# The four step-size features of a hybrid decoder trunk, computed on four column strips of TensorE

## The chip, the cores and the metric

The kernel runs on one core of a Trainium2 chip. The metric is the device time of one execution in microseconds (us), taken as the median of several runs. PE is TensorE, DVE is VectorE, ACT is ScalarE, POOL is GpSimd and SP is the engine whose queue issues the transfers. All data are fp32 in memory.

## The reference

One inference step runs through a two-layer decoder trunk. There are 1048 tokens: 16 meta tokens, a prompt of 1024 and 8 decode tokens, each with 1024 features. In each layer one input projection feeds three groups of mixers (attention, a diagonal state space called S5, and a Mamba-2 scan called SSD). Its last four columns are the raw step sizes of the four SSD heads:

```python
h = rmsnorm(x, ln1_g)
proj = h @ w_in                        # 1024 -> 1796 columns
q, k, v, u, z, xbc, dtr = split(proj)  # dtr: the last 4 columns
dt = softplus(dtr + ssd_dt_bias)       # step sizes of the 4 SSD heads
cs = cumsum(dt * A)                    # A = -exp(ssd_a_log)
Lmat = exp(segment sums of cs)         # decays inside a chunk
```

After the mixers come an output projection, a second norm and a SwiGLU block of 2816 hidden features.

## The kernel before, in words

Features lie on the 128 partitions and tokens along the free dimension. The tokens are cut into two halves (528 and 520 tokens), and each half into two chunks of 264 or 256 tokens. So a layer has two halves and the kernel goes four times through the input projection. They are called (layer, half): (0,0), (0,1), (1,0) and (1,1).

Precision is kept by splitting. A dense product splits weights and activations each into a rounded fp32r part and a remainder; `mm3` (lines 206 to 213) then issues three fp32r matmuls for each of the eight 128-feature tiles of the contraction. `weights` (lines 176 to 187) loads a 128-column weight tile of 512 KB and splits it on ACT (line 184) and DVE (line 186).

`in_norm` (lines 303 to 316) makes the two parts of x times the norm gain, for each chunk and tile (lines 312 and 313), and the reciprocal norm `rs` of each token. The sum over features for that norm goes through PE at line 242 and comes back as a row at line 255. `in_proj` (lines 318 to 357) walks over the names in `MT` (line 33), one 128-column tile each, and multiplies each product by `rs` on the way out of PSUM (lines 347 and 351). The name "dt" holds the four step-size columns, padded to 128. It has its own weights: `weights_dt` (lines 189 to 199) casts the raw tile twice on ACT and writes the remainder of the four columns into columns 32 to 35. Its loop (lines 334 to 341) issues 16 fp32r matmuls per chunk, all 128 columns wide, copies rows 32 to 35 out on ACT, adds rows 0 to 3 and multiplies by `rs` on DVE. The result of 4 rows is stored to a DRAM buffer.

`ssd` loads these 4 rows back and turns them so that tokens are on partitions: five transposes of 4 rows (lines 891 and 896), then a short DVE chain makes the softplus.

All instructions pass through a list scheduler that runs while the program is built. It goes by program order, lifted where `tc.high_priority` stands, and by a simulated timeline; the order on each engine is then fixed. PE takes matmuls in that order, and SP issues all transfers in that order. Buffers rotate in pools: PSUM has two banks for dense products (`pbig`), three for general use (`pmx`) and three for attention; `st` staging tiles are three, general slots 28. At the top (lines 1486 to 1533) the parts are strung together: in layer 0, (0,0) and (0,1) are mixed with the preparation of S5 and with mixers; in the rest the mixers are woven into the dense SwiGLU work. In program order `in_norm(0,0)`, `in_norm(0,1)` and `in_norm(1,1)` stand ahead of the dense work that runs next, and `in_norm(1,0)` stands behind the output projection of (0,1).

Of the kernel before, what the change touches and what calls it, by code (L numbers as in the profile page):

```python
# [7 lines left out]
F32 = mybir.dt.float32  # L8
F32R = mybir.dt.float32r
BF16 = mybir.dt.bfloat16  # L10
AF = mybir.ActivationFunctionType
ALU = mybir.AluOpType
AX = mybir.AxisListType
# [11 lines left out]
TH = (528, 520)  # L25
T0 = (0, 528)
NPR = (528, 512)
CH = (((0, 264), (264, 528)), ((0, 264), (264, 520)))
# [1 line left out]
NK8 = (66, 64)  # L30
HGROUPS = ((0, 8), (8, 16), (16, 22))
EPS = 1e-6
MT = 'u0 u1 k v q0 q1 q2 q3 xs0 xs1 B C dt z0 z1'.split()


def build(ctx, tc, A):
    nc = tc.nc
    V, S, G, PE = nc.vector, nc.scalar, nc.gpsimd, nc.tensor
# [4 lines left out]
    wp = ctx.enter_context(tc.tile_pool(name="wp", bufs=3))  # L43
    stp = ctx.enter_context(tc.tile_pool(name="stp", bufs=3))
# [10 lines left out]
    def nm(s):  # L55
        uid[0] += 1
        return f"{s}_{uid[0]}"
# [54 lines left out]
    def dram(shape, s):  # L112
        return drp.tile(shape, F32, tag=nm("d" + s), name=nm("d" + s))
# [6 lines left out]
    def load(out, in_):  # L120
        last[0] = nc.sync.dma_start(out=out, in_=in_).ins  # L121
        return last[0]
# [11 lines left out]
    ident = const([128, 128], "id")  # L134
# [32 lines left out]
    x = [None, None]  # L167
# [8 lines left out]
    def weights(src, nk, parts=1):  # L176
        raw = wp.tile([128, 8, 128], F32, tag="wr", name=nm("wr"), bufs=2)
        with tc.high_priority(offset=3000):
            load(raw[:, 0:nk], src)
        wh = wp.tile([128, 8, 128], F32R, tag="wh", name=nm("wh"))  # L180
        wl = wp.tile([128, 8, 128], F32R, tag="wl", name=nm("wl"))
        cuts = [nk * i // parts for i in range(parts + 1)]
        for a, b in zip(cuts, cuts[1:]):
            S.copy(wh[:, a:b], raw[:, a:b])  # L184
        for a, b in zip(cuts, cuts[1:]):
            V.tensor_sub(wl[:, a:b], raw[:, a:b], wh[:, a:b].bitcast(F32))  # L186
        return wh, wl

    def weights_dt(l, mi):

        raw = wp.tile([128, 8, 128], F32, tag="wr", name=nm("wr"), bufs=2)
        with tc.high_priority(offset=3000):
            load(raw, A["w_in"][l, mi])
        wh = wp.tile([128, 8, 128], F32R, tag="wh", name=nm("wh"))
        S.copy(wh, raw)
        wl = wp.tile([128, 8, 128], F32R, tag="wl", name=nm("wl"))
        S.copy(wl, raw)
        V.tensor_sub(wl[:, :, 32:36], raw[:, :, 0:4], wh[:, :, 0:4].bitcast(F32))
        return wh, wl

    def split(dst, cols, src, eng=None):
        h, l = dst[:, 0, cols], dst[:, 1, cols]
        S.copy(h, src)  # L203
# [27 lines left out]
    def rstd_sum(acc, n, scale, out=None):  # L231
        rs = ftp.tile([128, 264], F32, tag="rs", name=nm("rs")) if out is None else out
        S.copy(rs[:, :n], rstd_rows(acc, n, scale))
        return rs
# [52 lines left out]
    P = {}  # L287
    for l in range(DEPTH):
        for hf in range(2):
            T = TH[hf]  # L290
            for n_ in ("xs0", "xs1", "B", "C", "k", "v", "z0", "z1"):
                P[l, hf, n_] = dram([128, T], n_)
            P[l, hf, "dt"] = dram([4, T], "dt")
            P[l, hf, "u"] = dram([2, 128, 8 * NK8[hf]], "u")
            P[l, hf, "ud"] = dram([2, 128, NDEC], "ud")
            P[l, hf, "q"] = dram([4, 128, T], "q")
            P[l, hf, "mixa"] = dram([4, 128, T], "mixa")
            for j in range(4):
                P[l, hf, f"mix{j}"] = P[l, hf, "mixa"][j]
            for j in range(4, 8):  # L300
                P[l, hf, f"mix{j}"] = dram([128, T], "mix")

    def in_norm(l, hf, new):

        xn = [new() for _ in range(8)]
        g = par("ln1", l)
        rs = slot()
        for c0, c1 in CH[hf]:
            acc = None
            for k, t in enumerate(x[hf]):  # L310
                h, lo = xn[k][:, 0, c0:c1], xn[k][:, 1, c0:c1]
                S.activation(h, t[:, c0:c1], AF.Copy, scale=g[:, k:k + 1])
                V.scalar_tensor_tensor(lo, t[:, c0:c1], g[:, k:k + 1], h.bitcast(F32), ALU.mult, ALU.subtract)  # L313
                acc = add_square(acc, t[:, c0:c1], c1 - c0)
            rstd_sum(acc, c1 - c0, 1.0 / D, rs[:, c0:c1])
        return xn, rs

    def in_proj(l, hf, xr, early=0):

        xn, rs = xr  # L320
        bn = [0]
        T = TH[hf]
        nk = NK8[hf]
        for mi, name in enumerate(MT):
            w = weights(A["w_in"][l, mi], 8) if name != "dt" else weights_dt(l, mi)
            st = stp.tile([128, 528], F32, tag="st", name=nm("st"))
            for c0, c1 in CH[hf]:
                n = c1 - c0
                bn[0] += 1
                if mi < early and bn[0] % 2:  # L330
                    ps = mxp.tile([128, 512], F32, tag="xa", name=nm("px"), bufs=PSB["a"])
                else:
                    ps = pbig()
                if name == "dt":
                    for k in range(8):
                        PE.matmul(ps[:, :n], w[1][:, k, :], xn[k][:, 0, c0:c1], start=(k == 0), stop=False)
                        PE.matmul(ps[:, :n], w[0][:, k, :], xn[k][:, 1, c0:c1], start=False, stop=(k == 7))
                    S.copy(st[0:4, c0:c1], ps[32:36, :n])
                    V.tensor_add(st[0:4, c0:c1], st[0:4, c0:c1], ps[0:4, :n])
                    V.tensor_mul(st[0:4, c0:c1], st[0:4, c0:c1], rs[0:4, c0:c1])  # L340
                    continue
                mm3(ps[:, :n], w, xn, c0, c1)
                if name[0] == "u":
                    e = min(c1, NPR[hf])
                    sv = st[:, 0:8 * nk].rearrange("p (s k) -> p k s", s=8)
                    by8 = lambda t: t.rearrange("p (k s) -> p k s", s=8)
                    V.tensor_mul(sv[:, c0 // 8:e // 8, :], by8(ps[:, :e - c0]), by8(rs[:, c0:e]))
                    if e < c1:
                        V.tensor_mul(st[:, e:c1], ps[:, e - c0:n], rs[:, e:c1])
                else:  # L350
                    V.tensor_mul(st[:, c0:c1], ps[:, :n], rs[:, c0:c1])  # L351
            with tc.high_priority(offset=3000):
                if name == "dt":
                    load(P[l, hf, "dt"], st[0:4, :T])
                elif name[0] == "u":
                    load(P[l, hf, "u"][int(name[1])], st[:, :8 * nk])
                    if T > 8 * nk:
                        load(P[l, hf, "ud"][int(name[1])], st[:, 8 * nk:T])
                elif name[0] == "q":
                    load(P[l, hf, "q"][int(name[1])], st[:, :T])  # L360
                else:
                    load(P[l, hf, name], st[:, :T])
            yield
# [469 lines left out]
    def ssd(l, hf):  # L833
        T, NP = TH[hf], NPR[hf]
# [46 lines left out]
        f0 = 16 if hf == 0 else 0  # L881
        blocks += [(f0 + 128 * i, 128, i) for i in range(4)]

        dr = slot()
        load(dr[0:4, :T], P[l, hf, "dt"])
        sm5 = kvp.tile([128, 9, 20], F32, tag="ssds", name=nm("ssds"), bufs=2)
        v_, e_, s_, z_, dt, dA, cs, w_, mx_ = [sm5[:, i, :] for i in range(9)]
        V.memset(v_, 0.0)
        pt = pmx()
        for i in range(4):  # L890
            PE.transpose(pt[:, 4 * i:4 * i + 4], dr[0:4, f0 + 128 * i:f0 + 128 * i + 128], ident[0:4, 0:4])
        V.tensor_copy(v_[:, 0:16], pt[:, 0:16])
        pt2 = pmx()
        ne = 16 if hf == 0 else 8
        o5 = 0 if hf == 0 else NP
        PE.transpose(pt2[0:ne, 0:4], dr[0:4, o5:o5 + ne], ident[0:4, 0:4])
        V.tensor_copy(v_[0:ne, 16:20], pt2[0:ne, 0:4])
        b5 = lambda n: par(n, l).unsqueeze(1).to_broadcast([128, 5, 4])
        f5 = lambda t: t.rearrange("p (b h) -> p b h", h=4)
# [53 lines left out]
        for c0, nq, bi in blocks:  # L953
            cols = slice(c0, c0 + nq)
# [602 lines left out]
def _host(i):  # L1557
    import numpy as np

    c = np.ascontiguousarray  # L1560
    f = np.float32
    r = {}
# [4 lines left out]
    cols = {"k": np.arange(512, 640), "v": np.arange(640, 768), "u0": np.arange(768, 896), "u1": np.arange(896, 1024),  # L1567
            "z0": np.arange(1024, 1152), "z1": np.arange(1152, 1280), "xs0": np.arange(1280, 1408),
            "xs1": np.arange(1408, 1536), "B": np.arange(1536, 1664), "C": np.arange(1664, 1792),
            "dt": np.arange(1792, 1796)}  # L1570
    for j in range(4):
        cols[f"q{j}"] = hp[128 * j:128 * j + 128]
    wcols = {n: i["w_in"][:, :, cols[n]] for n in MT}

    wcols["dt"] = np.concatenate([wcols["dt"], np.zeros((2, 1024, 124), f)], axis=2)

    def tiles(w, nm_):

# [11 lines left out]
    P = {}  # L1590
# [38 lines left out]
    st = np.stack([i["state_s5_re"], i["state_s5_im"]], axis=1)  # L1629
# [75 lines left out]
```

## Time and profile before

| | us |
|---|---|
| median of 3 runs | 2483.13 (2478.48 to 2488.88) |
| the profiled execution | 2487.19 |
| its span, first to last instruction | 2485.3 |
| PE busy in it | 2396.9 (96%) |
| DVE busy | 1463.9 (59%) |
| ACT busy | 1059.1 (43%) |

The rows further down come from that one profiled execution. A matmul's own duration in the trace contains its way through the array, and matmuls overlap; the pace of PE is read from the distance between the starts of neighbours. A plain fp32 product appears as two matmuls in the trace (two passes), a fp32r product or a transpose as one.

### The profile page before, as it was taken

Reading aid. Unit: us, or ns where it says so; the run is one execution under the profiler, and the core shown is the slowest. Engines: PE = TensorE matmul, PEld = TensorE weight load, DVE = VectorE, ACT = ScalarE, POOL = GpSimd, SP = SyncE. Lnnn points to the kernel's source line nnn. Section 1 sums busy time; section 2 is a strip of 40 time slices with the busy share of each in tenths; the row PEclk is TensorE's granted clock in tenths of the full one; section 3 lists DMA queues with packets and bytes.
Section 4 is the critical chain, followed back from the end, with each engine's and each line's share of the span. In section 5 each row is a group of like instructions: output and inputs, shape, how many; then the busy total and the mean of one; then the engine's idle time right before and its main releaser. Section 6 shows DMA issues by size and latency. Waiting matters only on the chain.

```text
span 2485.3 us, 49901 instructions
## 1 busy us (share of the span) xinstructions
PE 2396.9 (96%) x20006; PEld 2312.5 (93%) x20006; DVE 1463.9 (59%) x3502; ACT 1059.1 (43%) x2183; POOL 353.4 (14%) x478
## 2 busy tenths in 40 slices
PE   7999789999999999999999999999999999999997
PEld 7988688999999999999999999999999998999997
DVE  8777557666659655564664545665565447434344
ACT  5455534334543533353554443343454435323234
POOL 6302121011013230001110021001110004000000
PEclk9999899999999999999999999999999999999999
DMA  7555332454324534253432334446432233232322
GB/s 251 189 160 155 99 118 74 127 154 147 91 82 143 182 110 150 77 148 114 129 103 86 100 101 134 121 134 189 139 100 89 84 117 111 95 94 89 99 83 80
DMA packets 202712, 301.09 MB, mean 121 GB/s; under 512 B 55905, under 2 KB 132529, under 8 KB 202449
## 3 DMA queue, kind: packets, MB, share of 16 engines
q1 hardware_dynamic: 202480, 297.91, 38.7%
q8 instruction: 157, 2.57, 0.4%
q14 instruction: 75, 0.61, 0.1%
HBM read 255.86 MB, written 46.17 MB: 122 GB/s over the span
## 4 chain that ended last, share of the span: by engine, by line
PE 77%; DVE 10%; issue 5%; DMA 4%; ACT 3%; SPq 1%; POOL 1%; DVEq 0%; POOLq 0%; ACTq 0%
PE pb L211 22%; PE pb L212 22%; PE pb L213 22%; DVE wl L186 2%; PE px L1250 1%; PE px L1205 1%; DVE xn L265 1%; SPq L121 1%; DVE hh L204 1%; ACT wh L184 1%; PE px L1253 1%; PE px L1234 1%; PE px L814 1%; PE px L255 1%; PE px L1235 1%
## 5 line engine op out<-in xcount | busy, mean ns | idle before, releaser
L211 PE MATMUL pb<-hh,wh 128*128 128x264 f32 (+1 forms) x3200 | 918.1, 287 | 17.6 <-DVE th L1420 15.6
L212 PE MATMUL pb<-hh,wh 128*128 128x264 f32 (+1 forms) x3200 | 913.5, 286 | 0.9 <-DVE hh L204 0.9
L213 PE MATMUL pb<-hh,wl 128*128 128x264 f32 (+1 forms) x3200 | 910.3, 285 | 0.0
L211 PE MATMUL pb<-hl,wh 128*128 128x264 f32 (+1 forms) x2304 | 660.6, 287 | 17.1 <-DVE st L351 6.7
L212 PE MATMUL pb<-hl,wh 128*128 128x264 f32 (+1 forms) x2304 | 657.8, 286 | 0.5 <-DVE hl L313 0.5
L213 PE MATMUL pb<-hl,wl 128*128 128x264 f32 (+1 forms) x2304 | 656.4, 285 | 0.0
L184 ACT CAST wh<-wr 128x512 fp32r<-128x512 f32 (+2 forms) x536 | 387.1, 753 | 574.8 <-PE pb L212 527.9
L211 PEld LDWEIGHTS pb<-hh,wh 128*128 128x128 f32 x3200 | 606.6, 190 | 26.9 <-DVE th L1420 20.0
L213 PEld LDWEIGHTS pb<-hh,wl 128*128 128x128 f32 x3200 | 606.3, 189 | 4.1 <-issue 3.3
L212 PEld LDWEIGHTS pb<-hh,wh 128*128 128x128 f32 x3200 | 605.2, 189 | 4.9 <-issue 2.1
L186 DVE TENSOR_TENSOR wl<-wr,wh 128x512 fp32r<-128x512 f32 (+2 forms) x536 | 462.5, 884 | 181.9 <-ACT wh L184 175.5
L211 PEld LDWEIGHTS pb<-hl,wh 128*128 128x128 f32 x2304 | 436.0, 189 | 27.3 <-issue 10.3
L212 PEld LDWEIGHTS pb<-hl,wh 128*128 128x128 f32 x2304 | 435.5, 189 | 3.4 <-issue 1.7
L213 PEld LDWEIGHTS pb<-hl,wl 128*128 128x128 f32 x2304 | 436.0, 189 | 1.8 <-issue 1.5
L228 POOL TENSOR_TENSOR sq<-sq,sq 128x264 f32<-128x264 f32 (+1 forms) x142 | 117.9, 835 | 684.1 <-ACT sq L225 596.0
L1421 DVE SCALAR_TENSOR_TENSOR th<-th,pb 128x264 f32<-128x264 f32 (+1 forms) x176 | 74.6, 424 | 143.2 <-PE pb L213 142.2
L1436 DVE TENSOR_TENSOR x<-x,pb 128x264 f32<-128x264 f32 (+1 forms) x176 | 74.4, 423 | 142.1 <-PE pb L213 141.0
L203 ACT CAST hl<-th 128x264 fp32r<-128x264 f32 (+1 forms) x176 | 71.8, 408 | 191.8 <-DVE th L1421 191.6
L1420 DVE SCALAR_TENSOR_TENSOR th<-th,pb 128x264 f32<-128x264 f32 (+1 forms) x176 | 74.2, 422 | 77.7 <-ACT th L1419 77.2
L1419 ACT ACTIVATE th<-pb 128x264 f32<-128x264 f32 (+1 forms) x176 | 67.7, 385 | 98.8 <-PE pb L213 98.2
L225 ACT ACTIVATE sq<-x 128x264 f32<-128x264 f32 (+1 forms) x160 | 63.8, 416 | 103.9 <-DVE x L1400 61.7
L204 DVE TENSOR_TENSOR hl<-th,hl 128x264 fp32r<-128x264 f32 (+1 forms) x176 | 81.5, 463 | 28.3 <-ACT hl L203 27.5
(426 smaller groups left out, 2602.1 us busy)
## 6 DMA issues: line engine op xcount, KB each, us to landing
wr<-w_gate SPq DMA_DIRECT2D x88, 512.0 KB, 3.2
wr<-w_up SPq DMA_DIRECT2D x88, 512.0 KB, 3.4
wr<-w_down SPq DMA_DIRECT2D x64, 512.0 KB, 3.6
wr<-w_in SPq DMA_DIRECT2D x60, 512.0 KB, 3.3
wr<-w_out SPq DMA_DIRECT2D x32, 512.0 KB, 3.3
wr<-w_down SPq DMA_DIRECT2D x32, 384.0 KB, 3.2
x<-xt SPq DMA_DIRECT2D x48, 132.0 KB, 3.8
s<-ds5v SPq DMA_DIRECT2D x16, 256.0 KB, 3.7
```

The costliest lines, as they stand in the source:

```text
L184: S.copy(wh[:, a:b], raw[:, a:b])
L186: V.tensor_sub(wl[:, a:b], raw[:, a:b], wh[:, a:b].bitcast(F32))
L203: S.copy(h, src)
L204: (eng or V).tensor_sub(l, src, h.bitcast(F32))
L211: PE.matmul(ps, wh[:, k, :], ah, start=(k == order[0]), stop=False)
L212: PE.matmul(ps, wh[:, k, :], al, start=False, stop=False)
L213: PE.matmul(ps, wl[:, k, :], ah, start=False, stop=(k == order[-1]))
L228: (eng or G).tensor_tensor(acc[:, :n], acc[:, :n], sq[:, :n], ALU.add)
L1419: S.activation(th[:, :n], pg[:, :n], AF.Tanh, scale=0.5)
L1420: V.scalar_tensor_tensor(th[:, :n], th[:, :n], 1.0, pg[:, :n], ALU.add, ALU.mult)
L1421: V.scalar_tensor_tensor(th[:, :n], th[:, :n], 0.5, pu[:, :n], ALU.mult, ALU.mult)
L1436: V.tensor_add(x[hf][m][:, c0:c1], x[hf][m][:, c0:c1], ps[:, :n])
```

## The change

The name "dt" leaves `MT`, and `weights_dt` with its loop in `in_proj` goes. At the end of `in_norm`, for each half, the four columns are loaded for all eight feature tiles as a 128 x 8 x 32 tile (28 of each 32 columns are zero), multiplied by the norm gain on DVE, and used as stationary operand of plain fp32 products of x itself. For each chunk there are eight products of 32 columns: feature tile 4q+j goes to column strip j (PSUM partitions 32j to 32j+31), and the two q of a strip add up there. DVE multiplies by `rs`, and four stores put 4 rows of each strip into a DRAM buffer that now has 16 rows. In `ssd` the 16 rows come back, and each of the five transposes becomes a plain fp32 product with a 16 x 4 matrix (made by a small DVE reduction of the identity) that turns the tokens to partitions and adds the four strips in one.

```diff
-MT = 'u0 u1 k v q0 q1 q2 q3 xs0 xs1 B C dt z0 z1'.split()
+MT = 'u0 u1 k v q0 q1 q2 q3 xs0 xs1 B C z0 z1'.split()
...
-    def weights_dt(l, mi):
-
-        raw = wp.tile([128, 8, 128], F32, tag="wr", name=nm("wr"), bufs=2)
-        with tc.high_priority(offset=3000):
-            load(raw, A["w_in"][l, mi])
-        wh = wp.tile([128, 8, 128], F32R, tag="wh", name=nm("wh"))
-        S.copy(wh, raw)
-        wl = wp.tile([128, 8, 128], F32R, tag="wl", name=nm("wl"))
-        S.copy(wl, raw)
-        V.tensor_sub(wl[:, :, 32:36], raw[:, :, 0:4], wh[:, :, 0:4].bitcast(F32))
-        return wh, wl
...
-            P[l, hf, "dt"] = dram([4, T], "dt")
+            P[l, hf, "dt"] = dram([16, T], "dt")
...
+        wdt = slot()[:, 0:256].rearrange("p (k m) -> p k m", k=8)
+        load(wdt, A["w_dt"][l])
+        V.tensor_mul(wdt, wdt, g.unsqueeze(2).to_broadcast([128, 8, 32]))
+        st = stp.tile([128, 528], F32, tag="st", name=nm("st"))
+        for c0, c1 in CH[hf]:
+            ps = pmx()
+            for q in range(2):
+                for j in range(4):
+                    PE.matmul(ps[32 * j:32 * j + 32, :c1 - c0], wdt[:, 4 * q + j, :], x[hf][4 * q + j][:, c0:c1],
+                              start=(q == 0), stop=(q == 1))
+            V.tensor_mul(st[:, c0:c1], ps[:, :c1 - c0], rs[:, c0:c1])
+        for j in range(4):
+            load(P[l, hf, "dt"][4 * j:4 * j + 4], st[32 * j:32 * j + 4, :TH[hf]])
         return xn, rs
...
-            w = weights(A["w_in"][l, mi], 8) if name != "dt" else weights_dt(l, mi)
+            w = weights(A["w_in"][l, mi], 8)
...
-                if name == "dt":
-                    for k in range(8):
-                        PE.matmul(ps[:, :n], w[1][:, k, :], xn[k][:, 0, c0:c1], start=(k == 0), stop=False)
-                        PE.matmul(ps[:, :n], w[0][:, k, :], xn[k][:, 1, c0:c1], start=False, stop=(k == 7))
-                    S.copy(st[0:4, c0:c1], ps[32:36, :n])
-                    V.tensor_add(st[0:4, c0:c1], st[0:4, c0:c1], ps[0:4, :n])
-                    V.tensor_mul(st[0:4, c0:c1], st[0:4, c0:c1], rs[0:4, c0:c1])
-                    continue
...
         dr = slot()
-        load(dr[0:4, :T], P[l, hf, "dt"])
+        load(dr[0:16, :T], P[l, hf, "dt"])
+        s16 = small()
+        V.tensor_reduce(s16[0:16, 0:4], ident[0:16, 0:16].rearrange("p (j h) -> p h j", h=4), axis=AX.X, op=ALU.add)
...
-            PE.transpose(pt[:, 4 * i:4 * i + 4], dr[0:4, f0 + 128 * i:f0 + 128 * i + 128], ident[0:4, 0:4])
+            PE.matmul(pt[:, 4 * i:4 * i + 4], dr[0:16, f0 + 128 * i:f0 + 128 * i + 128], s16[0:16, 0:4], start=True, stop=True)
...
-        PE.transpose(pt2[0:ne, 0:4], dr[0:4, o5:o5 + ne], ident[0:4, 0:4])
+        PE.matmul(pt2[0:ne, 0:4], dr[0:16, o5:o5 + ne], s16[0:16, 0:4], start=True, stop=True)
```

## Rows read from the trace of the kernel before

**Rows 1.** The page: PE's busy time, and its granted clock in 40 slices (tenths).
```profile
PE 2396.9 (96%) x20006; PEld 2312.5 (93%) x20006; DVE 1463.9 (59%) x3502; ACT 1059.1 (43%) x2183; POOL 353.4 (14%) x478
...
PEclk9999899999999999999999999999999999999999
```

**Rows 2.** The page: the chain that ended last, by engine, then by line.
```profile
PE 77%; DVE 10%; issue 5%; DMA 4%; ACT 3%; SPq 1%; POOL 1%; DVEq 0%; POOLq 0%; ACTq 0%
PE pb L211 22%; PE pb L212 22%; PE pb L213 22%; DVE wl L186 2%; PE px L1250 1%; PE px L1205 1%; DVE xn L265 1%; SPq L121 1%; DVE hh L204 1%; ACT wh L184 1%; PE px L1253 1%; PE px L1234 1%; PE px L814 1%; PE px L255 1%; PE px L1235 1%
```

**Rows 3.** Stretches: length, busy us of PE, PEld, DVE, ACT, POOL; clock; DMA.
```profile
0.00:320.00 320.00, 278.81 (x2230) 256.40 (x2231) 237.81 (x678) 170.77 (x370) 91.20 (x127) 0.93 0.55 172
...
990.00:1500.00 510.00, 506.90 (x4288) 487.02 (x4288) 280.75 (x654) 225.69 (x475) 57.98 (x73) 1.00 0.35 107
```

**Rows 4.** Timeline of PE (start, duration): the dt matmuls of (1,0), first and next.
```profile
975.43 0.28 PE L336 MATMUL pb<-hl,wl 128*128 128x264 f32 x1
...
979.33 0.28 PE L211 MATMUL pb<-hl,wh 128*128 128x264 f32 x1
```

**Rows 5.** Timeline of PE: two adjoining strips of 64 columns between full-width matmuls.
```profile
242.35 0.28 PE L212 MATMUL pb<-hl,wh 128*128 128x264 f32 x1
...
242.57 0.43 PE L1250 MATMUL px<-hs,hs 128*64 128x256 f32 x1
...
242.57 0.43 PE L1253 MATMUL px<-hs,hs 128*64 128x256 f32 x1
...
242.83 0.38 PE L1250 MATMUL px<-hs,hs 128*64 128x256 f32 x1
242.84 0.80 PE L1253 MATMUL px<-hs,hs 128*64 128x256 f32 x3
...
243.57 0.38 PE L1205 MATMUL px<-ckp,hr 128*128 128x256 f32 x1
```

**Rows 6.** Timeline of PE: full-width plain fp32 products, three of two passes.
```profile
547.85 1.49 PE L814 MATMUL px<-s,s 128*128 128x264 f32 x6
```

**Rows 7.** Timeline of PE: one 64-column fp32 product alone, and its follower.
```profile
239.45 0.65 PE L1250 MATMUL px<-hs,hs 128*64 128x256 f32 x2
240.02 0.51 PE L1205 MATMUL px<-ckp,hr 128*128 128x256 f32 x2
```

**Rows 8.** Timeline of PE: the turns of dt, with the matmuls around them.
```profile
192.82 0.28 PE L213 MATMUL pb<-hl,wl 128*128 128x256 f32 x1
193.03 0.41 PE L891 MATMUL px<-cid,s 4*128 4x4 f32 x4
...
193.39 0.38 PE L211 MATMUL pb<-hl,wh 128*128 128x256 f32 x1
```

**Rows 9.** Timeline of PE: eight plain fp32 products of 8 columns, and their follower.
```profile
589.13 1.84 PE L1308 MATMUL px<-m,s 128*128 128x8 f32 x16
590.83 0.37 PE L211 MATMUL pb<-hh,wh 128*128 128x264 f32 x1
```

**Rows 10.** Timeline of PE: norm sums of (1,0) twice, then those of (1,1).
```profile
877.82 0.24 PE L242 MATMUL px<-cones,sq 128*88 128x1 f32 x2
...
883.75 0.24 PE L242 MATMUL px<-cones,sq 128*88 128x1 f32 x2
...
1445.92 0.56 PE L242 MATMUL px<-cones,sq 128*88 128x1 f32 x6
```

**Rows 11.** Timeline of PE: two waits of the first stage (idle before, releaser in brackets).
```profile
35.96 0.36 PE L211 MATMUL pb<-hl,wh 128*128 128x264 f32 x1 [2.54 <-DVE st L347]
...
102.38 0.41 PE L621 MATMUL px<-s,s 128*128 128x32 f32 x2 [2.06 <-DVE s L594]
```

**Rows 12.** The stretch behind the second of these waits, columns as in Rows 3.
```profile
102.90:109.70 6.80, 6.49 (x38) 6.18 (x37) 5.46 (x16) 3.35 (x13) 4.20 (x4) 0.50 0.57 196
```

**Rows 13.** By line: the dt casts, copies and multiplies (min/median/max ns).
```profile
L195 ACT CAST wh<-wr x4: 1047/1048/1055, 84.7 to 1551.4; 128x1024 fp32r<-128x1024 f32 x4
...
L338 ACT COPY st<-pb x8: 363/371/372, 104.5 to 1566.9; 4x264 f32<-4x264 f32 x6, 4x256 f32<-4x256 f32 x2
...
L340 DVE TENSOR_TENSOR st<-st,s x8: 406/414/420, 107.3 to 1569.2; 4x264 f32<-4x264 f32 x6, 4x256 f32<-4x256 f32 x2
```

**Rows 14.** Timeline of SP: the store of the dt rows of (0,1).
```profile
243.11 0.29 SPq L121 DMA_DIRECT2D ddt<-st  x1
```

More of the change, by code (lines that the diff above doesn't have):

```diff
@@ L352, in in_proj @@
             with tc.high_priority(offset=3000):
-                if name == "dt":
-                    load(P[l, hf, "dt"], st[0:4, :T])
-                elif name[0] == "u":
+                if name[0] == "u":
                     load(P[l, hf, "u"][int(name[1])], st[:, :8 * nk])
@@ L1573, in _host @@
     wcols = {n: i["w_in"][:, :, cols[n]] for n in MT}
-    wcols["dt"] = np.concatenate([wcols["dt"], np.zeros((2, 1024, 124), f)], axis=2)
+    wdt = i["w_in"][:, :, cols["dt"]].reshape(2, 8, 128, 4).transpose(0, 2, 1, 3)
+    r["w_dt"] = c(np.concatenate([wdt, np.zeros((2, 128, 8, 28), f)], axis=3).astype(f))
     def tiles(w, nm_):
```

## Prediction

> **What bounds the kernel now.** I read the page from the top. PE is busy for 2396.9 of 2485.3 us, and its granted clock stands at the upper level (2.4 GHz) in nearly every slice [rows 1]. The chain that ended last runs through PE for 77% of the span, two thirds of the span in the three lines of `mm3` [rows 2]; nothing else holds more than 10%. So what counts is PE time, and ACT, DVE or DMA work only where PE waits for it. The stretches differ, though. From 990 to 1500 us PE is busy 506.9 of 510.0 us: a microsecond of PE taken there is a microsecond of the end. In the first 320 us it is busy 278.8 and its mean clock is 0.93 [rows 3]: there PE also waits, for DVE evictions at 35.96 us and for the S5 preparation at 102.38 us [rows 11], and a microsecond taken from it may only become waiting. Two of the four step-size products, (0,0) and (0,1), lie in that first stretch; (1,0) and (1,1) lie where PE is full.
>
> **The change part by part.**
>
> *The old products go.* Per half there are 2 chunks x 16 = 32 full-width fp32r matmuls. In (1,0) the first starts at 975.43 and the next tile's first matmul at 979.33 [rows 4]: 3.9 us for 32, or 0.122 each. Four halves: 4 x 3.9 = 15.6 us of PE. In (0,0) a part of them fell into a stretch at half clock, 1.2 GHz [rows 12], right behind a PE wait of 2.06 us [rows 11], and cost more; but that is the stretch with spare PE time, so I leave it at 3.9.
>
> *The new products come.* The trace has no strips of 32 columns; the nearest row is the pair of 64-column strips that attention uses with plain fp32. There the first passes of two products, one on each strip, start together at 242.57, their second passes together at 242.83, and a third product on one of the strips adds its two passes; the next full-width matmul starts at 243.57 [rows 5]. So strips overlap fully, and what is left in a row is four passes: 243.57 - 242.57 = 1.00 us. Entering costs 242.57 - 242.35 = 0.22 against the usual 0.12, so 0.10 more. A chunk of the change is the same figure: two products behind each other on each strip, so four passes in a row, at 264 columns instead of 256: 1.00 x 264/256 + 0.10 = 1.13 us. Eight chunks: 9.0 us. Bounds: below, four passes at the full-width pace without entering or leaving, where six passes fit into 1.49 us, (1.49 - 0.38)/5 = 0.222 each [rows 6], 0.89 a chunk or 7.1 us in all; above, no overlap at all, 16 x 0.222 + 0.2 = 3.75 a chunk or 30 us. I take 9.0, since the pair of strips is the nearest row.
>
> *The turns in `ssd`.* Five transposes now take from 192.82 to 193.39, less one normal step of 0.12: 0.45 us [rows 8]. Each becomes a plain fp32 product of two passes with few columns. The nearest row has 16 such passes between 589.13 and 590.83, 0.106 each [rows 9]: 10 x 0.106 + about 0.14 at the borders = 1.2, so +0.75 a half, +3.0 us in all. Lower bound: the passes run at the pace of the transposes now, (193.39 - 193.03)/5 = 0.07, which makes 0.7 + 0.1 and +1.4 us in all. I take 3.0: the stationary side is 128 columns of plain fp32 in both.
>
> *ACT and DVE.* Gone are two casts of 1.05 us a half and eight copies of 0.37 on ACT, and two DVE steps of 0.41 for each of eight chunks [rows 13]. New on DVE are one multiply by `rs` a chunk (the same length, 0.41), and for each half a scaling of 128 x 256 (at most 0.41, from the same row) and a tiny reduction. Both engines end with less work, off the path where PE is full; I cost it at nothing there, and the cover is the dense work of PE beside it. If it paid anywhere it would be in the first 320 us, where DVE is busy 237.8 us; at most it gives back the waits of [rows 11].
>
> *Transfers.* A 512 KB weight load and one store go per half; a small load and four stores come, three issues more, and the old store took 0.29 us of SP [rows 14]: about 1 us of SP's time a half. SP is in order: behind a store that waits for DVE's multiply by `rs` stand the next weight loads, and PE's dense products wait for those. The cover is that a weight tile of 48 matmuls lasts PE 5.9 us (883.75 - 877.82, two norm sums with 48 matmuls between them [rows 10]). Bound: 0 to one wait of 2.5 us, the size of the first row of [rows 11], in the first half; I take 0.
>
> *New waits on PE.* A product that stands in PE's order before its scaled weights are there holds all that is queued behind it, in (0,0) the first dense products. The likely place of the two bursts of (0,0) is between 16 and 34 us, ahead of the wait of 2.54 us at 35.96 [rows 11], which could swallow their 2.3 us. So -2.3 to +2.5; I take 0. The new chunk also holds a general PSUM bank until `rs` is there, one of three; nearest row again the 2.5 us.
>
> *The sum.* -15.6 + 9.0 + 3.0 = -3.6 us of PE. The part that lies in (0,0) and (0,1), about half, may be paid out only in part. I carry about -3. Against the profiled execution, 2487.2, that is 2484; this execution is 4.1 us above the median of the runs shown, 2483.1, and from the median the forecast is 2480.
>
> **The rivals.**
>
> *The products stand alone (slower).* The gain rests on eight products side by side. The scheduler also fills gaps with single instructions: norm sums of (1,0), which stand behind an output projection in program order, were issued one at a time with 48 dense matmuls between them, while those of (1,1) stand together [rows 10]. A lone fp32 product on a strip takes 240.02 - 239.45 = 0.57 us plus 0.10 for entering [rows 7, 5], 0.67 instead of 0.14 within a burst: +0.53 each. Seven of the 64 alone eat the 3.6 us; 30 alone make the kernel 0.5% slower; all 64 would cost 64 x 0.67 = 43 us instead of 9, so +30, 2513. From the rows I expect it for part of (1,0) only, some 5 products or +2.6, inside my range; half of all, 2496 to 2500, is what this rival stands for.
>
> *The strips don't overlap (slower).* If four strips of 32 behave other than two of 64, a burst costs up to 3.75 us, 30 in all: -15.6 + 30 + 3 = +17.4, 2500. Against it speak [rows 5].
>
> *Half an overlap (no change).* If each product's second pass has to come before the next strip's first may start, a burst is a chain of nine steps, 9 x 0.222 + 0.2 = 2.2 us, 17.6 in all: -15.6 + 17.6 + 3.0 = +5, 2488. In [rows 5] the second strip didn't wait for the first one's second pass, though in the code the first product stands wholly ahead of the second; but that is two strips. The Trainium skill ("TensorE: Matmul & The Clock Gate", Part 3, "The mechanism") says that matmuls start and end strictly in program order, without reordering; by that rule this would be the outcome, and the two starts at 242.57 do not fit it unless the two passes were already laid alternately.
>
> *The change is hidden.* The PE time taken in the first stretch turns into waits of the kind of [rows 11], and the 3 us of the turns stay: between -1 and +1 us, 2483.
>
> *The clock (faster).* In the first 320 us the mean clock is 0.93 [rows 3], which is 2 x 0.07 x 320 = 45 us at the lower level; the drop that covers 102.90 to 109.70 comes right behind a PE wait next to the dt products of (0,0) [rows 11, 12]. If the new order removes 18 of these 45 us, it gains 9 more: -12.6, 2470.5. From there on the kernel counts as faster. The reverse, 9 us lost, would leave it within half a per cent.
>
> **How the numbers follow.** Bursts with overlap, 2480: 0.50. Half an overlap, 2488: 0.14. Hidden, 2483: 0.12. Clock, 2470 and below: 0.09. Alone, 2496 and above: 0.08. No overlap, 2500: 0.07. The order of all other work is laid out anew, which I price by the waits of the first stretch, some 5 us either way. Half a per cent, 12.4 us, is about what a measurement of this kernel can tell from no change. Faster by more: 0.09 of the clock case and 0.04 of the first, 0.13. Slower by more: 0.08 + 0.07, and 0.02 each of the first and of the half overlap, 0.19. Within: 0.68. The range goes from 2468 (clock case, or the low bounds of burst and turns with a good order) to 2498 (half an overlap with a bad order, or half of the products alone); beyond it I leave 0.05 below and 0.13 above.
>
> **What would show it.** In the profile after: bursts of eight products, eight first passes and eight second ones, spanning about 1.0 us with four starts within some 20 ns; if the starts are spread by 0.22 us, the overlap is the step that fails. Single strip products between dense ones show the first rival; count them. The turns should take 1.2 us instead of 0.57 between their neighbours. ACT loses 11.4 us (8.4 of casts and 3.0 of copies). The first 320 us tell by their clock and PE's idle time whether hiding or the clock decided. The prediction is wrong if PE's busy time falls by 3 to 4 us and the time goes another way, or if PE gains work.

## The result, and the profile after

The changed kernel takes 2506.97 us (median of 4 runs, 2502.97 to 2509.33) against 2481.45 for the kernel before (4 runs, 2478.48 to 2488.88): a ratio of 1.0088, 95% interval 1.0067 to 1.011. The quotient of these two medians is 1.0103; against the medians that the kernel before had in later and larger samples (2486.51 to 2487.08, below) it is 1.008. The change makes this kernel about 0.9% slower. The forecast was 2480 with a range of 2468 to 2498; the measured time lies above the range. The profiled execution took 2507.48 us, its span is 2505.5.

The page of the changed kernel: PE's line, its granted clock in 40 slices, the chain that ended last by engine.

```profile
PE 2404.2 (96%) x20026; PEld 2309.5 (92%) x20026; DVE 1472.7 (59%) x3498; ACT 1046.8 (42%) x2165; POOL 358.1 (14%) x478
...
PEclk9999799999999999999999989999999999999998
...
PE 80%; DVE 10%; DMA 3%; ACT 3%; issue 2%; SPq 1%; POOL 1%; DVEq 0%; POOLq 0%; ACTq 0%
```

PE's busy time rose by 7.3 us [rows 1] where the sum said minus 3.6, and the span rose by 20.2. The clock row has an 8 in the middle, near 1470 us, where before there were only 9s [rows 1]. So I cut the span there. Stretches of the changed kernel, columns as in [rows 3]: length, busy us of PE, PEld, DVE, ACT, POOL, granted clock, DMA share, GB/s.

```profile
0.00:320.00 320.00, 275.54 (x2239) 249.59 (x2240) 239.18 (x675) 165.17 (x362) 95.49 (x127) 0.93 0.55 170
...
1400.00:1500.00 100.00, 84.63 (x666) 79.15 (x665) 45.36 (x78) 37.55 (x69) 13.79 (x18) 0.91 0.30 94
...
1443.00:1475.00 32.00, 16.63 (x96) 11.28 (x95) 15.31 (x29) 15.11 (x32) 6.06 (x8) 0.73 0.32 97
```

The same two of the kernel before:

```profile
1400.00:1500.00 100.00, 98.42 (x824) 98.04 (x823) 53.65 (x93) 47.09 (x88) 23.16 (x29) 1.00 0.33 105
...
1443.00:1475.00 32.00, 32.00 (x271) 31.88 (x271) 17.68 (x31) 16.86 (x34) 10.04 (x12) 1.00 0.28 92
```

The first 320 us hold no more PE work than before [rows 3]. From 1443 to 1475 PE was full before (271 matmuls); now it stands idle for 32.00 - 16.63 = 15.4 us, does 96 matmuls, and has a mean clock of 0.73. To see that nothing else counts, I numbered the 16,896 dense matmuls of `mm3` in both traces and took the start of each after minus before. Up to number 9,000 (at 1428.7 us, -0.2) every 250th lies within -3.2 to +5.0 us (single ones, up to 9 off, where the first stretch has another order); it is +24.9 at number 9,250, and +19.9 at the last. The whole loss is one place, the norm of (1,1) and the start of the output projection of (1,0). PE there, changed kernel (start, duration; idle before and releaser in brackets):

```profile
1443.52 0.63 PE L230 MATMUL px<-cones,sq 128*88 128x1 f32 x6 [0.44 <-POOL sq L216]
1450.76 1.25 PE L243 MATMUL px<-dg,cones 88*128 88x264 f32 x2 [6.61 <-DVE dg L235]
1454.62 1.01 PE L230 MATMUL px<-cones,sq 128*128 128x1 f32 x4 [2.62 <-POOL sq L216]
1456.73 1.20 PE L243 MATMUL px<-dg,cones 128*128 128x256 f32 x2 [1.10 <-DVE dg L235]
1457.86 3.68 PE L314 MATMUL px<-x,s 128*32 128x264 f32 x32
1461.47 0.50 PE L199 MATMUL pb<-hh,wh 128*128 128x256 f32 x2
...
1466.91 0.51 PE L199 MATMUL pb<-hh,wh 128*128 128x256 f32 x2 [2.71 <-ACT hh L191]
```

The brackets name the norm's own chain (DVE, POOL), but that chain is not new. Before, the norm sums of the first chunk stand at 1445.92 [rows 10] and their products 7.6 us later; those of the second chunk are 4.6 us apart:

```profile
1453.52 0.61 PE L255 MATMUL px<-dg,cones 88*128 88x264 f32 x2
...
1456.20 0.50 PE L242 MATMUL px<-cones,sq 128*128 128x1 f32 x4
...
1460.79 0.59 PE L255 MATMUL px<-dg,cones 128*128 128x256 f32 x2
```

PE was busy all that time with dense products of `out_proj(1, 0)`. What is new is that PE has nothing to do meanwhile. The row at 1466.91 says why: the dense products wait for `hh`, the cast of a mix tile, and the mix tiles come late. SP's queue, which issues their loads (`mo<-dmix`, `mo<-dmixa`), before:

```profile
1196.60 1.80 SPq L121 DMA_DIRECT2D mo<-dmix  x3
...
1406.77 0.33 SPq L121 DMA_DIRECT2D mo<-dmix  x1
1407.37 0.92 SPq L121 DMA_DIRECT2D mo<-dmixa  x2
...
1412.47 1.14 SPq L121 DMA_DIRECT2D mo<-dmixa  x2
```

and after:

```profile
1449.01 0.42 SPq L121 DMA_DIRECT2D s<-w_dt  x1
...
1449.96 0.90 SPq L121 DMA_DIRECT2D mo<-dmix  x2
1462.14 1.28 SPq L121 DMA_DIRECT2D ddt<-st  x4
1463.53 0.82 SPq L121 DMA_DIRECT2D mo<-dmix  x2
1464.68 5.30 SPq L121 DMA_DIRECT2D mo<-dmixa  x4
```

Before, all eight loads had gone by 1413.6, the first three of them near 1197; now the first two go at 1449.96, and six only behind the four stores of the step-size rows at 1462.14. The code says what ties them. The `st` pool has three buffers, and three places take from it under one tag: `in_proj`'s evictions, `out_proj`'s eight mix tiles (`mo`), and, since the change, the step-size rows in `in_norm`. In the program `nb = in_norm(1, 1, hl)` stands ahead of `out_proj(1, 0)`. Its `st` tile is thus asked for before the eight mix tiles, but can be filled only when x of the second half and its `rs` are final, and is free only when the four stores have read it. The mix tiles that PE's cover is made of have to pass it.

My theory (A in the expectations): the new tile's place in that pool, ahead of the mix tiles, takes away the cover of the norm of (1,1). The rivals that I weigh it against: the tile of the scaled weights (a general slot) or its load, which goes just ahead of the mix loads, holds SP's queue; the new products themselves cost more than the sum says where PE is full; the pool has too few buffers, whoever stands first.

### The profile page after: what moved, and what is told of

It reads as the page before. It is cut to its first block, busy times and chain, and to the rows that moved or that the text cites. A ratio compares the mean times of both kernels' runs of the same rounds, so it can differ in the third digit from the quotient of the medians.

```text
span 2505.5 us, 49916 instructions
## 1 busy us (share of the span) xinstructions
PE 2404.2 (96%) x20026; PEld 2309.5 (92%) x20026; DVE 1472.7 (59%) x3498; ACT 1046.8 (42%) x2165; POOL 358.1 (14%) x478
## 4 chain that ended last, share of the span: by engine, by line
PE 80%; DVE 10%; DMA 3%; ACT 3%; issue 2%; SPq 1%; POOL 1%; DVEq 0%; POOLq 0%; ACTq 0%
PE pb L199 23%; PE pb L200 23%; PE pb L201 23%; DVE wl L186 2%; PE px L1200 1%; PE px L1245 1%; DVE xn L253 1%; SPq L121 1%; ACT wh L184 1%; DMA mo<-dmixa 1%; PE px L807 1%; PE px L1229 1%; PE px L1248 1%; PE px L243 1%; PE px L1230 1%
```

## The experiments

Times are medians beside runs of the kernel before on the same chip (2486.88 us for e1 to e4, 2486.51 for e5 to e8, 2487.08 for e9), with the ratio and its 95% interval.

**e1: the step-size rows in another buffer.** In `in_norm`:

```diff
-        st = stp.tile([128, 528], F32, tag="st", name=nm("st"))
+        st = slot()
```

> The changed kernel, but the staging tile of the four features comes from the general slots and no longer from the three st buffers, out of which the output projection also takes its eight mix tiles. Theory A (the st buffers are handed out in program order; the new tile of (1,1) stands ahead of the eight mix tiles of the output projection of (1,0) and waits for x to be final, so the mix tiles come late and PE waits): the wait at 1443 to 1467 us goes, about 24 us, and the kernel comes to 2476 to 2484. Theory B (the load of the scaled weights waits for a general slot and holds SP's queue, the mix loads with it): unchanged, 2505 to 2509. Theory C (the price lies in the products and turns themselves, on PE): unchanged, 2505 to 2509.

Measured: 2488.11 us, 1.0001 (0.999 to 1.0012). One line of the change takes back the 0.9%. Its SP queue and its stretch:

```profile
1407.71 0.33 SPq L121 DMA_DIRECT2D mo<-dmix  x1
1408.31 0.92 SPq L121 DMA_DIRECT2D mo<-dmixa  x2
...
1412.78 1.45 SPq L121 DMA_DIRECT2D mo<-dmixa  x2
```

```profile
1400.00:1500.00 100.00, 98.72 (x843) 97.11 (x843) 52.50 (x91) 44.72 (x85) 22.98 (x29) 1.00 0.34 106
```

The mix loads are back at 1407 to 1413, PE is full and the clock at its upper level (2.4 GHz). The theory's place and mechanism hold; its time, 2476 to 2484, was a little too good, a point that comes back below.

**e4: the same tile, asked for later.** Only the step of (1,1) moves, behind the output projection:

```diff
     nb = in_norm(1, 1, hl)      # without the step sizes
     out_proj(1, 0)
+    in_dt(1, 1, nb[1])          # the step-size part of in_norm
```

> The changed kernel, but the new step of (1,1) alone (its weights, products, staging and stores) stands behind the output projection of (1,0) in program order instead of ahead of it; all buffers as in the changed kernel. Theory A (st buffers in program order): the wait goes, 2476 to 2484. Theory B (the weights' slot): goes as well, since that load stands behind too, 2476 to 2484. Theory C (products and turns): 2505 to 2509.

Measured: 2487.53 us, 1.0003 (0.9994 to 1.0013).

```profile
1403.63 0.33 SPq L121 DMA_DIRECT2D mo<-dmix  x1
...
1490.00 1.28 SPq L121 DMA_DIRECT2D ddt<-st  x4
```

The same pool, the same number of buffers, the same products: with the tile behind the mix tiles in program order the loss is gone. That speaks against too few buffers. It says nothing about the weights tile, whose place and load move along with the step; e3 and e2 settle that.

**e3: the kernel before, with nothing but the tile.** The full-width products stay; `in_norm(1, 1)` takes an `st` tile, writes four rows of squares of `rs` to it, and stores them where nobody reads:

```diff
+        if (l, hf) == (1, 1):
+            st = stp.tile([128, 528], F32, tag="st", name=nm("st"))
+            V.tensor_mul(st[0:4, :TH[hf]], rs[0:4, :TH[hf]], rs[0:4, :TH[hf]])
+            load(dram([4, TH[hf]], "hold"), st[0:4, :TH[hf]])
```

> The kernel before with nothing of the change, but at the end of the input norm of (1,1) one st tile is taken, written by one DVE multiply of the norm rows and stored to an unused buffer. Theory A (st buffers in program order): the wait of the changed kernel comes into the old one, 20 to 25 us more than before, 2502 to 2507. Theories B and C: within 2 us of before, 2480 to 2484.

Measured: 2506.96 us, 1.0083 (1.0068 to 1.0099). The tile alone makes the whole loss, without one new product and without the load of `w_dt`. SP and PE:

```profile
1449.57 0.90 SPq L121 DMA_DIRECT2D mo<-dmix  x2
1459.11 0.27 SPq L121 DMA_DIRECT2D dhold<-st  x1
1460.52 0.80 SPq L121 DMA_DIRECT2D mo<-dmix  x2
1461.44 5.49 SPq L121 DMA_DIRECT2D mo<-dmixa  x4
```

```profile
1450.85 1.25 PE L255 MATMUL px<-dg,cones 88*128 88x264 f32 x2 [6.61 <-DVE dg L247]
```

The longest wait is that of the changed kernel to the hundredth, 6.61 us. The new products and the load of `w_dt` fall as causes of the wait. From 1425 to 1475 us of the kernel before, the same dense matmuls last 21.7 us longer here, and 24.6 in the changed kernel, which has the products of (1,1) there too.

**e2: the scaled weights out of the general slots.**

```diff
-        wdt = slot()[:, 0:256]...
+        wdt = ftp.tile([128, 264], F32, tag="xn", name=nm("wd"), bufs=4)[:, 0:256]...
```

> The changed kernel, but the 128x256 tile of the step-size weights comes from a small buffer of the norms and no longer from the general slots; the staging tile stays in the st buffers. Theory A (st buffers in program order): unchanged, 2503 to 2510, with the PE wait near 1443 us still there. Theory B (the weights' slot holds SP's queue): the wait goes, 2476 to 2484. Theory C (products and turns): unchanged.

Measured: 2500.52 us (two runs), 1.0055 (1.0035 to 1.0075). The wait is still there, and the first mix tiles go at 1441.62, behind five weight loads. PE:

```profile
1442.90 1.25 PE L243 MATMUL px<-dg,cones 88*128 88x264 f32 x2 [6.61 <-DVE dg L235]
```

So the weights tile isn't what holds the mix tiles: between 1425 and 1475 us of the kernel before, the same dense matmuls last 24.2 us longer here, as good as the 24.6 of the changed kernel. That the kernel is still some 6 us faster than the changed one has another source: its trace is 10 us ahead of the kernel before at 300 us, 9 at 400 and 8 at 1428 (see e6 and e7).

**e8: a fourth `st` buffer** (two buffers of `xn` given up for the room).

```diff
-    stp = ctx.enter_context(tc.tile_pool(name="stp", bufs=3))
+    stp = ctx.enter_context(tc.tile_pool(name="stp", bufs=4))
...
-                xn = ftp.tile([128, 264], F32, tag="xn", name=nm("xn"), bufs=4)
+                xn = ftp.tile([128, 264], F32, tag="xn", name=nm("xn"), bufs=2)
```

> The changed kernel with four st buffers instead of three, so that the new tile of (1,1) leaves three for the mix tiles as before (room for it taken from the norms' buffers: two xn tiles instead of four). If what counts is the number of buffers: the wait near 1445 us goes, 2478 to 2490. If what counts is the order in which they are handed out: the mix tiles still come behind the new tile, 2500 to 2510.

Measured: 2499.69 us, 1.0064 (1.0047 to 1.0081).

```profile
1442.24 0.42 SPq L121 DMA_DIRECT2D s<-w_dt  x1
...
1443.19 1.37 SPq L121 DMA_DIRECT2D mo<-dmix  x3
1455.35 1.28 SPq L121 DMA_DIRECT2D ddt<-st  x4
```

With four buffers three mix tiles go ahead of the stores instead of two, as one more buffer lets them, but they too go late, and the rest still stands behind the stores. So the order decides, and one more buffer takes back only a small part. The median is some 7 us below that of the changed kernel, with overlapping intervals of the two ratios and with `xn` changed beside it; but in the trace this kernel is 6.7 us ahead of the changed one already at dense matmul 9,000, before the wait. Across the wait, up to number 10,000, it loses 21.1 us against the kernel before and the changed kernel 24.6, and up to number 9,250 it is 23.2 against 25.1. So the fourth buffer is worth some 2 to 4 us. Why even those mix tiles that have a buffer go only at 1441 to 1450 isn't explained by the count: in all four kernels with the wait (changed, e2, e3, e8) none of these loads goes near 1197, where three go in the kernel before and in e1, and all stand behind the same five weight loads in SP's queue. How the scheduler comes to that order stays open.

**e5: does the array's side-by-side work pay?** On top of e1, all eight products of a chunk go to one strip and are summed there; four rows are stored, and the transposes in `ssd` are as before the change.

```diff
-    PE.matmul(ps[32 * j:32 * j + 32, ...], ..., start=(q == 0), stop=(q == 1))
+    PE.matmul(ps[0:32, ...], ..., start=(q + j == 0), stop=(q + j == 4))
```

> The first experiment (staging tile in the general slots) with all eight products of a chunk on one strip of 32 columns, so that none can run beside another; the result has 4 rows, one store, and the five turns are transposes again. If the four strips overlap fully on the chip, as the starts 7 ns apart in the changed kernel say: a chunk takes 16 passes of 0.222 and 0.2 at the borders, 3.75 us instead of 1.13 (eight chunks: +21), and the transposes give 3 back: +18 us against the first experiment, of which the quarter that lies in (0,0) may be swallowed by a wait, so +12 to +18, 2499 to 2507 beside 2488. If the overlap bought nothing that reaches the end: 2484 to 2490.

Measured: 2500.85 us, 1.006 (1.0043 to 1.0076), 0.59% or 14.7 us above e1. The products of (1,0) on one strip:

```profile
910.92 4.19 PE L314 MATMUL px<-x,s 128*32 128x264 f32 x18
915.05 0.63 PE L230 MATMUL px<-cones,sq 128*88 128x1 f32 x6
915.61 3.30 PE L314 MATMUL px<-x,s 128*32 128x264 f32 x14
918.84 0.39 PE L199 MATMUL pb<-hl,wh 128*128 128x264 f32 x1
```

and in the changed kernel, on four:

```profile
903.33 1.52 PE L314 MATMUL px<-x,s 128*32 128x264 f32 x18
904.78 0.63 PE L230 MATMUL px<-cones,sq 128*88 128x1 f32 x6
905.34 1.09 PE L314 MATMUL px<-x,s 128*32 128x264 f32 x14
906.36 0.39 PE L199 MATMUL pb<-hl,wh 128*128 128x264 f32 x1
```

The same 32 passes last 4.13 + 3.23 = 7.36 us one behind the other and 1.45 + 1.02 = 2.47 us on four strips. Without the strips the change would be a loss even when the wait is mended.

**e9: how much of the new products is paid at all?** On top of e4 the products of the step sizes are left out; the step multiplies a tile of x by `rs` in place of them.

```diff
-            ps = pmx()
-            ...            # the eight products
-            V.tensor_mul(st[:, c0:c1], ps[:, :c1 - c0], rs[:, c0:c1])
+            V.tensor_mul(st[:, c0:c1], x[hf][0][:, c0:c1], rs[:, c0:c1])
```

> The fourth experiment (step of (1,1) behind the output projection) without the strip products: DVE multiplies the first feature tile of x by rs in place of the sum in PSUM, so the four features are not computed at all; weights load, scaling, staging, stores and turns stay. The profile of the fourth experiment has 2.7 us of PE time at the products of (1,0). If PE time is paid out everywhere: four halves, 2.7 x 4 = 11 us less than the fourth experiment, 2475 to 2479 where that one is at 2487, ratio to before about 0.996. If the products of (0,0) and (0,1) are hidden in the waits of the first stretch: only two halves count, 5.4 us less, 2480 to 2484, ratio about 0.998. If products are hidden everywhere: no change, ratio 1.000.

Measured: 2479.89 us, 0.9973 (0.9961 to 0.9986): 0.30% or 7.5 us below e4. The PE time of the products, at the 2.8 us a half measured in (1,0) (below), is 11.1 us in all and 5.5 for the two halves where PE is full. The 7.5 lie between, as if part of the first stretch's work were paid and part not; but the edges of the two intervals leave room for either end, so this isn't shown.

**e6 and e7: both remedies with e2's place for the weights.** e6 is e4 with the weights tile of e2, e7 is e1 with it.

> The step of (1,1) stands behind the output projection as in the fourth experiment, and the weights' tile lies in the norms' small buffers as in the second. The second experiment ran some 10 us ahead of the kernel before at 400 us and lost 24 of them at 1445. If the two are independent: both hold, 10 us less than before at 400 us and no wait at 1445, 2470 to 2478, below both kernels. If the lead in the first stretch was chance of one order: 2482 to 2490, no change.

> As the sixth, with the staging tile in the general slots (first experiment) instead of the step moved behind. If the two are independent: 2470 to 2478. If the lead of the second experiment in the first stretch hangs on its order there: 2482 to 2490. The theory that st buffers are handed out in program order wants no wait near 1445 us in either case.

Measured: e6 2478.65 us, 0.997 (0.9957 to 0.9983); e7 2484.84 us, 0.9998 (0.9989 to 1.0007). e6 beats both kernels, the one before by 7.9 us; in its trace it is 6.7 us ahead of the kernel before at 567 us and 9.7 at the end. The same weights tile brings nothing measurable in e7. So this gain seems to belong to one order of the first stretch and not to the weights tile as such. I looked for it in the time at the lower clock before 400 us, and that doesn't follow: 54.5 us in the kernel before, 51.0 in e2, but 64.7 in e6 and 54.6 in e7. What makes e2's and e6's first stretch shorter stays open.

## Why the prediction was wrong

**The step that failed** is "New waits on PE", with its neighbour "Transfers". The text asked who is held by the scaled weights and by a general PSUM bank, put the possible waits into the first half, with bounds of 2.5 us from [rows 11], and took 0. It didn't name the third thing that the change takes: a staging tile of the `st` pool. "Transfers" saw that loads stand behind the new stores in SP's queue, but thought of the next weight loads and their cover; what stood there were six mix loads. In place of that 0 the runs show 22 us at (1,1), where PE is full (worked out below; e3, with the tile alone, has 21.7). The right question would have been who takes the next tiles of that tag in the program. The answer, eight mix tiles of `out_proj(1, 0)`, stands a line below `in_norm(1, 1, hl)`, and the chain that the mix tiles cover was in the rows: the sums of (1,1) at 1445.92 stand together [rows 10]. A price was to be had too: in the trace of before the norm's two chunks of (1,1) take 7.6 us (1445.92 to 1453.52) and 4.6 us (1456.20 to 1460.79) from the sums to their products (rows above), so a full loss of the cover is some 12 us of idle time. The text read the same row only for how the scheduler places single instructions.

**What it cost.** From 1425 to 1475 us the same dense work lasts 24.6 us longer than before. 15.4 of that is idle PE. The rest is work, part of it at the lower clock (1.2 GHz): the 32 passes of the half take 3.6 us there (1457.86 to 1461.47), and the norm's sums and products and the first dense matmuls share what is left. The sum had 2 x 1.13 = 2.26 us for these products, so the term that it lacked is 24.6 - 2.3 = 22.3 us. Minus 3.6 plus 22.3 is +18.7; the spans differ by 20.2, and the median of the changed kernel lies 20 us above the later medians of the kernel before (25.5 above the one of the result's four runs).

**The terms that were there.** Measured as the time that the same dense matmuls take in the trace after, minus before, around each step of (1,0), with what was predicted:

| step of (1,0) | predicted us | measured us |
|---|---|---|
| old products gone (960 to 985) | -3.9 | -3.9 |
| new products (860 to 960) | +2.26 | +2.8 |
| turns in `ssd` (985 to 1010) | +0.75 | +0.75 |

The new products are 0.5 dearer. The 32 passes were laid as 18 and 14 with norm sums between them (the rows at 903.33 to 905.34), so the strips are entered twice, and the last product ahead of the norm sums has its two passes to itself:

```profile
904.24 0.61 PE L314 MATMUL px<-x,s 128*32 128x264 f32 x2
```

That makes ten steps of 0.222 instead of eight, 0.44 more. At (0,0), (0,1) and (1,1) the 32 stand together, and in e1 those of (1,1) make the dense work only 1.97 longer. At (0,0):

```profile
29.17 1.99 PE L314 MATMUL px<-x,s 128*32 128x264 f32 x32
```

Within the burst at 29.17 the four strips' first passes start some 0.007 us apart; the next four follow after 0.247 us and further groups of four every 0.222, four groups a chunk, as the text had it. The turns, in the changed kernel:

```profile
191.29 0.28 PE L201 MATMUL pb<-hl,wl 128*128 128x264 f32 x1
191.51 1.05 PE L886 MATMUL px<-m,s 16*128 16x4 f32 x8
...
192.62 0.39 PE L199 MATMUL pb<-hl,wh 128*128 128x264 f32 x1
```

From 191.29 to 192.62 is 1.33, less one step of 0.12: 1.21 us, predicted 1.2. ACT lost 1059.1 - 1046.8 = 12.3 us, predicted 11.4.

**The rivals.** *Alone*: no strip product stands between dense ones; the bursts of the changed kernel are 32, 32, 18 and 14, and 32 passes. One product of the 64, at 904.24, ran with none beside it, where the text expected some five. That rival's time (2496 and above) is nearer to the measured one than any other, but as the cause of it the mechanism didn't happen. *No overlap*: e5 made it, 7.36 us a half; the changed kernel has 2.47. *Half an overlap*: the starts 0.007 us apart rule it out here. The Trainium skill ("TensorE: Matmul & The Clock Gate", Part 3, "The mechanism") has matmuls start strictly in program order, by which this rival was worked out. Four products of two passes whose first passes start together don't fit that rule, unless the passes are laid alternately in the instruction stream, which no run here shows. *Clock*: before 400 us the time at the lower level went from 54.5 to 61.3 us instead of falling; the drop that counts is a new one at 1447.7, behind PE's wait. *Hidden*: with the wait mended (e1, e4) the change is worth 1.0001 and 1.0003, with intervals of 0.1% around them, where the sum says 0.9985. So this rival, 2483, is nearer than the 2480 that I took as likeliest: the PE time of the turns and products is spent where PE is full, as the table shows, and the table's terms leave (1,0) a gain of 0.4 us (-3.9 + 2.8 + 0.75) where the sum had 0.9; whether the gain in the first stretch is paid out whole, e9 leaves open. The single traces can't say where the 3.6 us went: the spans of e1 and e4 are 2.6 and 5.9 below that of the kernel before while their medians are equal to it (e4's profiled execution is the fastest of its ten). That stays open.

**The chances.** "Slower" had 0.19, and the wait that decided was not among the cases. The text's last sentence said that the prediction would be wrong if PE's busy time fell as predicted and the time went another way; in e1 and e4 it fell by 6.9 and 5.1 us. The other sign that it named, that PE gains work, is what the page of the changed kernel shows: 7.3 us more busy time, though the work is that of e1, part of it at the lower clock.

## What to carry to other kernels

A tile from a rotating pool is a place in a queue: ask who takes the next tiles of that tag in program order, what the new tile waits for before it is free, and whose cover comes through the pool; here one `st` tile, asked for one call too early, cost 22 us against a sum of 3.6 for all PE terms, and was mended by one line (e1) or by moving the step (e4). A chain of waits that costs nothing today, as the norm of (1,1), has its cover in other work: write down where that work's data come from before you add anything ahead of them. In the table, terms worked out from the nearest rows of PE were right to 0.5 us each, so what is to be feared is the term that isn't on the list.

## What the runs showed of the hardware

Four strips of 32 columns with plain fp32 overlap as fully as two of 64 did in [rows 5]: 18 passes on four strips in 1.45 us against 4.13 on one. I had left 0.21 for the cases without it.

The clock made the wait dearer than its idle time. Three stretches of the changed kernel:

```profile
1443.00:1450.00 7.00, 0.71 (x7) 0.54 (x6) 6.50 (x12) 6.97 (x16) 2.29 (x3) 0.84 0.18 54
1450.00:1457.00 7.00, 2.52 (x7) 1.72 (x8) 2.00 (x5) 2.32 (x8) 3.77 (x5) 0.50 0.49 159
1457.00:1461.50 4.50, 4.50 (x35) 1.63 (x34) 0.43 (x1) 1.41 (x3) 0.00 (x0) 0.51 0.00 0
```

PE had done nothing since 1444.1 when the granted clock fell to the lower level, at 1447.7, and the strip products that came then, busy throughout, ran at 0.51: their 32 passes lasted 3.68 us (the row at 1457.86), against 1.99 for the 32 that stand together at the upper level (the row at 29.17). The lower level was granted until 1461.4.
